# LP pooling over windows of four: the squares of loads 4, 8 and 12 in two parts, with the root and the store of the block before between them

## The chip, the cores and the metric

One core of one Trainium2 chip. The metric is the device time of one execution in microseconds (us), given as the median of several runs. Before the change it is 394.11 us, the median of 3 runs from 394.06 to 394.17.

The engines that matter here: ScalarE (ACT in the profile) takes squares and roots, VectorE (DVE) adds, SyncE (SP) issues loads and the last stores, and 16 DMA engines move the data between HBM and the on-chip memory SBUF. A matrix engine and GpSimd exist and have no part in this kernel.

## What is computed

The input is 32 x 256 x 4096 float32, p is 2 and the window is 4. Each output is the root of the mean of four squares:

```python
out_length = length // kernel_size
for i in range(out_length):
    start = i * kernel_size
    end = start + kernel_size
    window = np.abs(x[:, :, start:end]) ** p
    result[:, :, i] = (np.mean(window, axis=-1)) ** (1.0 / p)
```

134.22 MB are read and 33.55 MB written. Since windows never cross a row's end, the input may be treated as one flat list of numbers that is cut where it suits.

## The kernel before

**Tiling.** The flat input is spread over 128 partitions and cut into 20 loads. Loads 0 to 18 have 13184 columns a partition (`W`, 6592 KB in all), load 19 has 11648. There are three slots for loads in SBUF (`X_SLOTS`): load i lies in slot i mod 3, so load i + 3 can start only when load i's slot has been used up. The sums of a load, a quarter as wide (`R` = 3296 columns), go to one of four places in a tile `ot`, place i mod 4; with four loads' roots in it the whole tile is stored at once. So loads 0-3, 4-7, 8-11 and 12-15 are blocks, each with one store (numbers 0 to 3) of 6592 KB; loads 16 to 18 and load 19 are stored from a free slot as stores 4 and 5.

**Work on one load.** ScalarE squares the slot in place (`square`, L88). VectorE adds columns in pairs in place (`pairs`, L94) and then the pairs (`fours`, L98), into the load's place in `ot`. For loads 4, 8, 12 and 16 the sums go to a PSUM tile `st` instead, so that they need not wait for the store of the block before. ScalarE then takes the root, scaled by 1/4 (`root`, L101), several neighbouring places at a time where it can; for loads 4, 8 and 12 it reads `st` and writes `ot`. Sums of loads 5, 9 and 13 write a place of `ot` that the store of the block before still reads; these wait for that store to land.

**Order.** The order on each engine is the order of the calls, written by hand (`manual_schedule`); only waits are added by the framework. One loop runs over loads 0 to 16. In step i ScalarE squares load i; the table `behind` says which roots follow that square, the table `ahead` which come before it. For i = 4, 8 and 12 `ahead` puts the root of load i - 1 in front of the square, and since this root completes a block, `roots` issues that block's store right behind it on ScalarE's own DMA queue (L115, L85). VectorE then gets the pairs and fours of load i, and SP the issue of load i + 3 (L82), which waits for fours of load i. SP issues everything in order, so a load that waits holds those behind it. Behind the loop, store 3 is issued on SP, load 17 follows the same pattern, and loads 18 and 19 share their squares between VectorE and ScalarE; stores 4 and 5 go out on SP.

`implied` tells the framework that one wait is covered by others and need not be made. It issues nothing.

Of the kernel before, what the change touches and what calls it, by code (L numbers as in the profile page):

```python
# [1 line left out]

# [4 lines left out]


@with_exitstack
def kernel(  # L10
    ctx: ExitStack,
    tc: tile.TileContext,
    x: bass.AP,
    p: float,
    kernel_size: int,
    out: bass.AP,
):

    nc = tc.nc

    assert float(p) == 2.0, "kernel specialized for p == 2"
    k = int(kernel_size)  # L30
    assert k == 4, "kernel specialized for kernel_size == 4"

    P = nc.NUM_PARTITIONS
    fp32 = mybir.dt.float32
    Act = mybir.ActivationFunctionType
    add = mybir.AluOpType.add
    xf = x.rearrange("b c l -> (b c l)")
    of = out.rearrange("b c l -> (b c l)")
    total = xf.shape[0] // P

    W = 13184
    R = W // k
    X_SLOTS = 3
    LAST = total - 19 * W
    widths = [W] * 19 + [LAST]
    n = len(widths)
    assert 0 < LAST <= W and LAST % 16 == 0


    blocks = [[0, 1, 2, 3], [4, 5, 6, 7], [8, 9, 10, 11], [12, 13, 14, 15], [18, 16, 17], [19]]  # L50
    block_of = {i: b for b, group in enumerate(blocks) for i in group}
    block_width = [sum(widths[i] for i in group) for group in blocks]

    x_pool = ctx.enter_context(tc.tile_pool(name="x_pool", bufs=1))
    o_pool = ctx.enter_context(tc.tile_pool(name="o_pool", bufs=1))
    s_pool = ctx.enter_context(tc.tile_pool(name="s_pool", bufs=1, space=bass.MemoryType.PSUM))
    x_tiles = [x_pool.tile([P, W], fp32, name=f"xt{j}") for j in range(X_SLOTS)]
    o_tile = o_pool.tile([P, 4 * R], fp32, name="ot")
    first = o_pool.tile([P, 1], fp32, name="first")
    s_tile = s_pool.tile([P, 4096], fp32, name="st")  # L60
    ctx.enter_context(tc.manual_schedule())

    def rows(flat, b, div):
        at = sum(block_width[:b]) * P // div
        return flat[at:at + block_width[b] * P // div].rearrange("(p w) -> p w", p=P)


    free = x_tiles[17 % X_SLOTS]
    place = {i: o_tile[:, i % 4 * R:(i % 4 + 1) * R] for i in range(16)}
    place[18] = free[:, R:2 * R]  # L70
    place[19] = free[:, 0:LAST // k]
    place[16] = free[:, 2 * R:3 * R]
    place[17] = free[:, 3 * R:4 * R]
    held = [o_tile[:, :]] * 4 + [free[:, R:4 * R], place[19]]

    xs, loads, stores, sums = {}, {}, {}, {}

    def load(i):
        b = block_of[i]
        at = sum(widths[j] for j in blocks[b][:blocks[b].index(i)])  # L80
        xs[i] = x_tiles[i % X_SLOTS][:, 0:widths[i]]
        loads[i] = nc.sync.dma_start(out=xs[i], in_=rows(xf, b, 1)[:, at:at + widths[i]])  # L82

    def store(b, queue):
        stores[b] = queue.dma_start(out=rows(of, b, k), in_=held[b])  # L85

    def square(v):
        return nc.scalar.activation(out=v, in_=v, func=Act.Square)  # L88

    def pairs(v):  # L90

        q = v.rearrange("p (n j) -> p n j", j=k)
        h = v[:, 0:v.shape[1] // 2].rearrange("p (n j) -> p n j", j=2)
        return nc.vector.tensor_tensor(out=h, in0=q[:, :, 0:2], in1=q[:, :, 2:4], op=add)  # L94

    def fours(o, v):
        h = v[:, 0:v.shape[1] // 2].rearrange("p (n j) -> p n j", j=2)
        return nc.vector.tensor_tensor(out=o, in0=h[:, :, 0], in1=h[:, :, 1], op=add)  # L98

    def root(o, s):  # L100
        return nc.scalar.activation(out=o, in_=s, func=Act.Sqrt, scale=1.0 / k)  # L101

    summed = {i: s_tile[:, 0:R] if i in (4, 8, 12, 16) else place[i] for i in range(n)}

    def roots(*group):
        if len(group) == 1:
            root(place[group[0]], summed[group[0]])
        else:
            v = o_tile[:, group[0] % 4 * R:(group[-1] % 4 + 1) * R]
            r = root(v, v)  # L110
            if group[0] in (5, 9):

                implied(r, stores[block_of[group[0]] - 1])
        if group[-1] in (3, 7, 11):
            store(block_of[group[-1]], nc.scalar)  # L115

    def implied(later, earlier):

        tc.declare_no_dep(later.ins, earlier.ins, reason="implied by the other waits")

    for i in range(X_SLOTS):
        load(i)


    ahead = {4: (3,), 8: (7,), 12: (11,)}
    behind = {3: [(0, 1, 2)], 7: [(5, 6), (4,)], 11: [(9, 10), (8,)], 14: [(12,)], 15: [(13, 14)], 16: [(15,)]}

    root(first[:, :], nc.const_aps.tensor(1.0, (P, 1), fp32))
    for i in range(17):
        if i in ahead:  # L130
            roots(*ahead[i])
        s = square(xs[i])
        if i in (3, 7, 11):

            for earlier in sums[i - X_SLOTS]:
                implied(s, earlier)
        for group in behind.get(i, []):
            roots(*group)
        sums[i] = pairs(xs[i]), fours(summed[i], xs[i])
        if i + X_SLOTS < n:  # L140
            load(i + X_SLOTS)

    store(3, nc.sync)
    square(xs[17])
    pairs(xs[17])
    fours(summed[17], xs[17])
    later = {18: 4608, 19: 2000}

    def shared_square(i):
        v = xs[i][:, 0:later[i]]  # L150
        nc.vector.tensor_tensor(out=v, in0=v, in1=v, op=mybir.AluOpType.mult)  # L151
        square(xs[i][:, later[i]:widths[i]])

    def shared_pairs(i):
        implied(pairs(xs[i]), loads[i])

    shared_square(18)
    roots(16)
    roots(17)
    shared_pairs(18)  # L160
    fours(summed[18], xs[18])
    shared_square(19)
    roots(18)
    store(4, nc.sync)
    shared_pairs(19)
    fours(summed[19], xs[19])
    roots(19)
    store(5, nc.sync)


# [1 line left out]
_INS = ['x', 'p', 'kernel_size']  # L172
_OUTS = [((32, 256, 1024), 'float32')]

_NUMBERS = {'p': 2.0, 'kernel_size': 4}


# [26 lines left out]
```

## Time and profile before

| | |
|---|---|
| median of 3 runs | 394.11 us (394.06 to 394.17) |
| the profiled execution's own time | 393.96 us |
| its span (first to last instruction) | 392.2 us |
| ScalarE busy | 274.4 us (70%), 37 instructions |
| VectorE busy | 218.2 us (56%), 42 instructions |
| DMA | 167.77 MB, mean 428 GB/s over the span |
| one square of 13184 columns | 11.19 us |
| pairs, fours of such a load | 7.03 us, 3.59 us |
| root of 3296 columns, from `ot` | 2.95 us |
| ScalarE waiting for loads, in all | 90.9 us, 13 times |
| VectorE waiting for squares, in all | 144.3 us, 18 times |
| VectorE waiting for stores, in all | 17.1 us, 3 times |

An engine's row tells how long it was busy with instructions; issuing a DMA isn't counted. A DMA's row on a queue (SPq, ACTq) marks the issue, and the transfer itself goes on for many microseconds behind it. Landing is when its completion is told. In the rows of time the place in brackets is the engine's idle time before an instruction, and what ended it. Stretches are counted from the span's start.

### The profile page before, as it was taken

What the parts mean: (1) busy time and instruction counts of PE and PEld (TensorE: products, weight loads), DVE (VectorE), ACT (ScalarE), POOL (GpSimd) and SP (SyncE); (2) the same over time, 40 slices, a digit from 0 to 9 for tenths busy, and PEclk for the clock granted to TensorE, in tenths of its full rate; (3) what the DMA queues carried; (4) which work ended last, traced back from release to release, by engine and by line L of the source; (5) the groups of instructions that cost most, each with busy time, mean ns of one, the idle gap of its engine ahead of it and who ended that gap; (6) DMA issues with size and microseconds to landing.
All of it is one profiled execution on the core that took longest, in us unless ns stands there. A gap on an engine that the chain in (4) does not pass through costs nothing.

```text
span 392.2 us, 176 instructions
## 1 busy us (share of the span) xinstructions
DVE 218.2 (56%) x42; ACT 274.4 (70%) x37; POOL 0.2 (0%) x4
## 2 busy tenths in 40 slices
DVE  0008477490593374905942748069418485699980
ACT  1095685979950859799509597995098999969910
POOL 0000000000000000000000000000000000000000
DMA  8999999999999999999999999999999999999997
GB/s 344 430 430 441 436 436 441 436 436 387 430 430 430 430 430 430 430 436 430 446 441 452 446 441 436 430 430 430 430 430 430 430 430 430 430 428 438 430 413 342
DMA packets 3744, 167.77 MB, mean 428 GB/s; under 512 B 416, under 2 KB 416, under 8 KB 416
## 3 DMA queue, kind: packets, MB, share of 16 engines
q1 hardware_dynamic: 3312, 147.52, 87.4%
q10 hardware_dynamic: 432, 20.25, 11.9%
HBM read 134.22 MB, written 33.55 MB: 428 GB/s over the span
## 4 chain that ended last, share of the span: by engine, by line
DMA 43%; ACT 31%; DVE 23%; issue 0%; ACTq 0%; SPq 0%; DVEq 0%
DMA xt<-in_x_dram 43%; ACT xt L88 28%; DVE xt L94 14%; DVE ot L98 5%; DVE xt L98 3%; DVE xt L151 2%; ACT ot L101 2%; ACT xt L101 1%; ACTq L85 0%; SPq L82 0%; DVEq L94 0%
## 5 line engine op out<-in xcount | busy, mean ns | idle before, releaser
L88 ACT ACTIVATE xt<-xt 128x13184 f32<-128x13184 f32 (+2 forms) x20 | 216.7, 10847 | 92.2 <-DMA xt<-in_x_dram 90.9
L94 DVE TENSOR_TENSOR xt<-xt 128x6592 f32<-128x6592 f32 (+1 forms) x20 | 139.7, 6986 | 144.6 <-ACT xt L88 144.3
L98 DVE TENSOR_TENSOR ot<-xt 128x3296 f32<-128x3296 f32 x13 | 46.7, 3592 | 17.5 <-DMA out_dram<-ot 17.1
L101 ACT ACTIVATE ot<-ot 128x3296 f32<-128x3296 f32 (+2 forms) x8 | 37.2, 4656 | 7.0 <-DVE ot L98 7.0
L101 ACT ACTIVATE xt<-xt 128x3296 f32<-128x3296 f32 (+1 forms) x3 | 8.5, 2840 | 8.8 <-DVE xt L98 8.8
L98 DVE TENSOR_TENSOR st<-xt 128x3296 f32<-128x3296 f32 x4 | 14.4, 3600 | 0.1
L98 DVE TENSOR_TENSOR xt<-xt 128x3296 f32<-128x3296 f32 (+1 forms) x3 | 10.4, 3458 | 0.1
L101 ACT ACTIVATE ot<-st 128x3296 f32<-128x3296 f32 x3 | 8.7, 2899 | 0.0
L151 DVE TENSOR_TENSOR xt<-xt 128x4608 f32<-128x4608 f32 (+1 forms) x2 | 7.2, 3593 | 0.0
L101 ACT ACTIVATE xt<-st 128x3296 f32<-128x3296 f32 x1 | 2.9, 2899 | 0.0
L101 ACT ACT_TABLE_LOAD x1 | 1.3, 1283 | 0.7 <-PEq L185 0.7
L101 ACT ACTIVATE first<-const-float32-1.0 128x1 f32<-128x1 f32 x1 | 0.2, 203 | 0.0
L185 POOL MEMSET const-bfloat16-1.0<- 128x1 bf16 x1 | 0.1, 101 | 0.0
L185 POOL MEMSET const-uint8-127<- 128x1 uint8 x1 | 0.1, 101 | 0.0
L185 POOL MEMSET const-float32-0.0<- 128x1 f32 x1 | 0.1, 98 | 0.2 <-issue 0.2
L185 POOL MEMSET const-float32-1.0<- 128x1 f32 x1 | 0.1, 98 | 0.0
## 6 DMA issues: line engine op xcount, KB each, us to landing
xt<-in_x_dram SPq DMA_DIRECT2D x19, 6592.0 KB, 29.7
out_dram<-ot ACTq DMA_DIRECT2D x3, 6592.0 KB, 35.1
out_dram<-ot SPq DMA_DIRECT2D x1, 6592.0 KB, 37.0
xt<-in_x_dram SPq DMA_DIRECT2D x1, 5824.0 KB, 21.9
out_dram<-xt SPq DMA_DIRECT2D x1, 4944.0 KB, 16.1
out_dram<-xt SPq DMA_DIRECT2D x1, 1456.0 KB, 8.2
```

The lines of the kernel that those rows point to most:

```text
L88: return nc.scalar.activation(out=v, in_=v, func=Act.Square)
L94: return nc.vector.tensor_tensor(out=h, in0=q[:, :, 0:2], in1=q[:, :, 2:4], op=add)
L98: return nc.vector.tensor_tensor(out=o, in0=h[:, :, 0], in1=h[:, :, 1], op=add)
L101: return nc.scalar.activation(out=o, in_=s, func=Act.Sqrt, scale=1.0 / k)
L151: nc.vector.tensor_tensor(out=v, in0=v, in1=v, op=mybir.AluOpType.mult)
L185: nc = _bacc.Bacc("TRN2", target_bir_lowering=False, num_devices=1)
```

## The change

For loads 4, 8 and 12 the square is cut in two along its columns. ScalarE squares the first 8812, 8340 or 8160 columns, then takes the root of load i - 1 and issues the store of the block before, and then squares the remaining 4372, 4844 or 5024 columns. Before, the root and the store came first and the square was one instruction. The order on VectorE and SP, the sizes of all DMAs, and every other instruction stay as they are. The added calls of `implied` belong to waits that the cut would otherwise add.

```diff
-    ahead = {4: (3,), 8: (7,), 12: (11,)}
+    ahead = {4: 8812, 8: 8340, 12: 8160}
...
     for i in range(17):
         if i in ahead:
-            roots(*ahead[i])
-        s = square(xs[i])
+            halves = square(xs[i][:, 0:ahead[i]]), roots(i - 1), square(xs[i][:, ahead[i]:W])
+        else:
+            s = square(xs[i])
...
+        if i in (7, 11, 15):
+            implied(s, halves[0])
+            implied(s, halves[2])
         for group in behind.get(i, []):
             roots(*group)
         sums[i] = pairs(xs[i]), fours(summed[i], xs[i])
+        if i in ahead:
+            implied(sums[i][0], loads[i])
+            implied(sums[i][1], loads[i])
         if i + X_SLOTS < n:
             load(i + X_SLOTS)
+            if i in ahead:
+                implied(loads[i + X_SLOTS], loads[i])
...
-        square(xs[i][:, later[i]:widths[i]])
+        return square(xs[i][:, later[i]:widths[i]])
...
-    shared_square(18)
+    s = shared_square(18)
+    implied(s, halves[0])
+    implied(s, halves[2])
```

On ScalarE the order around load 4 becomes, in the built program: square of load 3, roots of loads 0 to 2, first part of the square of load 4, root of load 3, issue of store 0, second part of the square of load 4, square of load 5. The first part waits for load 4, the root for VectorE's sum of load 3, the issue for the root; the second part has no wait of its own. Around loads 8 and 12 the pattern is the same, with the roots of loads 5, 6 and 4 (9, 10 and 8) in front.

## The prediction

> **What bounds the kernel now.** I read the slices of the span first, to see which resource is never idle, then the DMA queues, then the DMA rate by stretches, then the order of time around the first store, and last who waits for whom.
>
> ```profile
> ACT  1095685979950859799509597995098999969910
> ...
> DMA  8999999999999999999999999999999999999997
> GB/s 344 430 430 441 436 436 441 436 436 387 430 430 430 430 430 430 430 436 430 446 441 452 446 441 436 430 430 430 430 430 430 430 430 430 430 428 438 430 413 342
> ...
> q1 hardware_dynamic: 3312, 147.52, 87.4%
> q10 hardware_dynamic: 432, 20.25, 11.9%
> ```
>
> The reader is to see that ScalarE has holes in every group of loads and that the DMA engines have none: the two queues' packets take 87.4 + 11.9 = 99.3% of 16 engines' span. q10 is ScalarE's queue, with stores 0, 1 and 2; everything else is on q1. The kernel is a DMA stream, with compute fitted into its shadow. The same by stretches (columns: stretch, its length, busy time of VectorE, ScalarE and GpSimd, granted clock, DMA share, GB/s):
>
> ```profile
> 4.00:92.00 88.00, 42.47 (x8) 56.78 (x7) 0.00 (x0) 1.00 1.01 435
> 92.00:100.00 8.00, 0.00 (x0) 8.00 (x1) 0.00 (x0) 1.00 1.00 382
> 100.00:372.00 272.00, 167.29 (x33) 205.50 (x28) 0.00 (x0) 1.00 1.00 435
> ```
>
> Outside one stretch of 8 us the rate stands at 435 GB/s. There it is 382, so 8 x (1 - 382/435) = 0.97 us of transfer time is lost. The packet records agree: 20 packets that start between 91 and 98 us take 2.0 to 3.3 us where the usual packet of 52,736 bytes takes 1.947, and the excess over 16 engines is 0.97 us. They begin 0.9 us after the first DMA that ScalarE's queue ever issues, and are nearly all packets of loads. Stores 1 and 2 show none. At 372 us nothing has been lost but this and the start.
>
> Now the work around store 0, in order of time (start, duration, engine, line, operation, idle time before and what ended it):
>
> ```profile
> 77.05 8.43 ACT L101 ACTIVATE ot<-ot 128x9888 f32<-128x9888 f32 x1
> 77.17 7.03 DVE L94 TENSOR_TENSOR xt<-xt 128x6592 f32<-128x6592 f32 x1 [4.94 <-ACT xt L88]
> 84.23 3.59 DVE L98 TENSOR_TENSOR ot<-xt 128x3296 f32<-128x3296 f32 x1
> 87.86 2.95 ACT L101 ACTIVATE ot<-ot 128x3296 f32<-128x3296 f32 x1 [2.38 <-DVE ot L98]
> 90.84 0.38 ACTq L85 DMA_DIRECT2D out_dram<-ot  x1
> 91.27 22.27 ACT L88 ACTIVATE xt<-xt 128x13184 f32<-128x13184 f32 x2 [0.46 <-ACT ot L101]
> ...
> 126.95 3.59 DVE L98 TENSOR_TENSOR ot<-xt 128x3296 f32<-128x3296 f32 x1 [6.36 <-DMA out_dram<-ot]
> 128.82 11.19 ACT L88 ACTIVATE xt<-xt 128x13184 f32<-128x13184 f32 x1 [15.29 <-DMA xt<-in_x_dram]
> 140.05 7.03 DVE L94 TENSOR_TENSOR xt<-xt 128x6592 f32<-128x6592 f32 x1 [9.50 <-ACT xt L88]
> ```
>
> ScalarE idles 2.38 us until VectorE's sum of load 3 is there, takes the root, issues store 0, and only then squares load 4, which landed at 81.5. Later it waits 15.29 us for load 6. VectorE waits 6.36 us for store 0 before it may overwrite load 1's place with the sum of load 5, and 9.50 us more before it has work again. Both engines have slack behind the change; the DMA engines have none.
>
> **The change part by part.** Three places are alike; the first is worked in full.
>
> *Squares in two.* Whole squares give the price by width: 13184 columns 11.19 us, 9648 columns 8.24, 8576 columns 7.35, so 0.832 ns a column. For 8812 columns that is 7.35 + 236 x 0.000832 = 7.55 us, for 4372 it is 3.85: together 11.40, or 0.22 more than whole. At loads 8 and 12 it is 7.16 + 4.25 and 7.01 + 4.40, 11.41 each. Three times 0.22 is 0.65 us more ScalarE work, hidden by the 15.29, 14.74 and 14.71 us of ScalarE waiting for loads 6, 10 and 14; without that cover it would cost 0.65.
>
> *The move.* The first part begins where ScalarE now idles: its roots end at 77.05 + 8.43 = 85.48 and it overlaps the one before by some 0.1, so 85.39 to 92.94. The root follows to 95.79 and the issue of store 0 stands at 95.82 instead of 90.84: **4.98 us later**. The second part runs from about 96.25 to 100.1, where the whole square ended at 102.46: **2.4 us earlier**. At loads 8 and 12 the store goes from 169.29 to 173.93 (4.64 later) and from 247.15 to 251.64 (4.49 later), and the square ends 2.3 earlier. The store is the only DMA that this queue issues there.
>
> *What the earlier square gives.* The sums of load 4 end 2.4 us earlier, so SP issues load 7 at about 110.9 instead of 113.2. But load 6 holds the queue until it lands at 128.8, and load 7 waits there for 15 us already. Likewise for loads 11 and 15. Gain 0; the cover would have to go altogether before the 2.4 us counted.
>
> *What the later store costs.* Issue to landing took 36.0, 35.1 and 34.9 us for the three stores, against 15.6 for a load that has the engines to itself: a store shares them half and half with the loads. So it lands at 95.82 + 36.0 = 131.8, then 209.0 and 286.5. Three things wait for it. VectorE's sum of load 5 (L98) runs 131.9 to 135.5; behind it on VectorE stand the sums of load 6, released by a square that now ends at 140.0 and by the changed shares perhaps 2 us sooner, at about 138. VectorE still has at least 2.5 of its 9.50 us. The slot's next load, number 8, is issued at 130.6 + 5.0 = 135.6; loads 12 and 16 at 208.1 + 4.6 = 212.8 and 285.8 + 4.5 = 290.3. The load ahead of each lands at 144.4, 222.2 and 300.1. So they are queued 8.8, 9.4 and 9.8 us ahead, where it was 13.8, 14.1 and 14.3. To be in time a DMA needs from issue to its first packet 1.0 us on an idle ring (load 0) and 3.3 to 3.8 on a busy one (the stores). I take 3.8, the worst: at least 5.0 us are spare. SP issues in order, and the load behind each is asked for more than 10 us later, so nothing else is held up. Cost 0.
>
> *Which transfers run when.* The same bytes move: what the store doesn't take in the first 5 us, load 5 takes, and lands sooner; later the store takes it back. With packets always waiting on one queue or the other the total is unchanged, so loads 7, 11 and 15 land as before, and all behind load 15 with them: loads 18 and 19 at 346.8 and 360.6, stores 4 and 5 issued at 371.77 and 383.2, the last landing at 391.3.
>
> *The 0.97 us at the first use of ScalarE's queue.* The trace doesn't tell if it belongs to the queue's first DMA or to the moment. Bounds: gone, -0.97; as it is, 0; again at another store as well, +0.97. I take 0, since it comes within 1 us of the first issue and stores 1 and 2 pass without it: the first DMA stays first.
>
> *A rule against the change.* Issuing the store later goes against the Trainium skill, "DMA: Bandwidth & Descriptors", section "Rules for kernel authors", whose line on overlap says to issue a DMA early and wait on it late. By that line at full price the delays would be 4.98 + 4.64 + 4.49 = 14.1 us, and the kernel 408; the row of 99.3% says that no engine is idle to profit from an earlier store, and the sum goes by the row.
>
> Sum against the profiled execution: 393.96 (span 392.2 and 1.76 around it) + 0 + 0 + 0 = 393.96. The median shown is 394.11, 0.15 higher with runs 0.11 apart; I forecast on the median: **394.1 us**.
>
> **The rivals.**
>
> *A, faster: the first-use loss goes.* If the slow packets belong to a store that starts in the midst of a load with another one queued, then issuing at 95.8, near the end of load 5, could spare them: 394.11 - 0.97 = 393.1. For it: they are packets of loads, not of the store. Against it: stores 1 and 2 also start in the midst of loads, without loss.
>
> *B, slower: the queue runs dry between loads.* Load 8 can't be issued before store 0 has landed and VectorE has added for 3.6 us. If load 7 has less left by then than that, the engines empty. It decides from 5.0 us beyond my landing time. Did the store get 0.40 of the engines rather than half, its 15.6 us of work would last 39 us instead of 31.2, landing 7.8 later: 2.8 us dry at each of three places, 394.1 + 8.4 = 402.5. For it: the move uses up a third of the lead. Against it: three stores so far took half, within 1.1 us of each other.
>
> *C, slower by a little: the loss comes twice.* 394.11 + 0.97 = 395.1, if a later issue meets more loads.
>
> *D, the change doesn't do what it says.* The second part could be held by a wait of its own. The built program has none: the first part waits for the load alone, the second for nothing. Were it so all the same, ScalarE's 15 us would take it: 394.1.
>
> **How the numbers follow.** The forecast, with D, gets 0.82, A 0.07, B 0.08, C 0.03. About 0.2% (0.8 us) is what a measurement of this kernel can tell from no change. A passes that bound only when nearly all of the loss goes, so of its 0.07 I count 0.05 as faster; B and C make slower 0.11; same is 0.84. The likeliest case alone has 393.8 to 394.4, the spread of runs and the small changes of rate; the bounds of the one unknown, A and C, widen it to 393.1 to 395.1, and only B is left out.
>
> **What would show it.** ScalarE's row of 8812 columns near 85.4 and its store near 95.8; sums of load 5 waiting some 13 us for the store; load 8 issued near 135.6; load 7 landing near 144.4 as now; 435 GB/s from 100 to 372 us; one stretch of about 380 GB/s, moved to about 97 to 105. I am wrong if a second stretch stands below 430, if load 7 or 8 lands over 1 us late, or if the last load lands over 1 us away from 360.6.

## The result and the profile after

The changed kernel takes 396.20 us, the median of 20 runs, against 394.08 us for the kernel before, also 20 runs: a ratio of 1.0053, with a 95% interval of 1.0041 to 1.0065. It is slower by 2.1 us. The forecast was 394.1 us, no change. As telling as the median is the scatter: the kernel before lies between 393.83 and 394.70, the changed one between 393.44 and 397.86. Of the 141 runs of the kernel before that stand beside this study's experiments, 140 lie between 393.75 and 395.36, and one took 398.12: it isn't wholly free of such scatter.

The profiled execution took 396.01 us with a span of 394.2 us, 2.0 more than before. First the slices and the queues of the changed kernel's page, then its DMA rate by the same three stretches as before (stretch, length, busy VectorE, ScalarE and GpSimd, clock, DMA share, GB/s):

```profile
DMA  8999999999999999999999999999999999999995
GB/s 342 428 428 433 455 439 439 439 444 433 417 433 428 428 433 428 428 428 428 423 439 444 433 449 444 439 433 428 428 428 428 428 428 428 428 454 408 428 447 224
...
q1 hardware_dynamic: 3312, 147.52, 86.8%
q10 hardware_dynamic: 432, 20.25, 11.9%
```

```profile
4.00:92.00 88.00, 42.47 (x8) 59.73 (x6) 0.00 (x0) 1.00 1.00 433
92.00:100.00 8.00, 0.03 (x1) 7.55 (x4) 0.00 (x0) 1.00 1.00 415
100.00:372.00 272.00, 165.90 (x32) 201.24 (x29) 0.00 (x0) 1.00 1.00 434
```

No hole has opened: the rate from 100 to 372 us is 434 GB/s, where it was 435, and the slow stretch at 92 us has become faster, 415 after 382. What stands out is the last slice: 224 GB/s, where it was 342. The transfers run on with part of the engines.

The same place as in the prediction, around store 0, in order of time:

```profile
76.94 8.43 ACT L101 ACTIVATE ot<-ot 128x9888 f32<-128x9888 f32 x1
85.27 7.53 ACT L88 ACTIVATE xt<-xt 128x8812 f32<-128x8812 f32 x1
92.71 2.93 ACT L101 ACTIVATE ot<-ot 128x3296 f32<-128x3296 f32 x1
95.67 0.37 ACTq L85 DMA_DIRECT2D out_dram<-ot  x1
96.09 14.93 ACT L88 ACTIVATE xt<-xt 128x4372 f32<-128x4372 f32 x2 [0.45 <-ACT ot L101]
...
126.61 11.19 ACT L88 ACTIVATE xt<-xt 128x13184 f32<-128x13184 f32 x1 [15.59 <-DMA xt<-in_x_dram]
130.72 3.59 DVE L98 TENSOR_TENSOR ot<-xt 128x3296 f32<-128x3296 f32 x1 [12.65 <-DMA out_dram<-ot]
137.83 7.03 DVE L94 TENSOR_TENSOR xt<-xt 128x6592 f32<-128x6592 f32 x1 [3.52 <-ACT xt L88]
144.27 11.19 ACT L88 ACTIVATE xt<-xt 128x13184 f32<-128x13184 f32 x1 [6.47 <-DMA xt<-in_x_dram]
```

All of this is as forecast: the store 4.8 us later, VectorE waiting 12.65 us for it and still 3.52 us idle behind it, load 7 there at 144.27. The time is lost behind these lines, and no view of engines and waits tells where. The trace's completion records do. Each transfer has 16 of them, one from each DMA engine, and it counts as landed with the last. First, middle (median) and last of the 16 completions, in us:

```
                 before                        changed
           first  middle    last         first  middle    last
load 4     80.51   80.87   81.52         80.60   80.99   81.40
load 8    159.30  159.66  159.96        158.75  159.11  159.81
load 11   221.56  221.92  222.24        221.01  221.36  223.37
load 15   299.40  299.76  300.08        298.85  299.21  301.54
load 19   359.95  360.31  360.62        359.39  359.74  362.57
store 5   390.68  391.03  391.33        390.13  390.47  393.37
```

In the changed kernel the middle engine ends 0.56 us *sooner* than before, and the last one 2.04 us later; the second-last ends at 390.81. One engine of sixteen has fallen behind, in steps: between loads 8 and 11, while store 1 ran, its lag behind the middle one grew by 1.3 us, and it grew further while stores 2 and 3 ran. The packet records show the same step. A full load is 128 packets of 52,736 bytes, 8 for each of the 16 engines, and a packet usually takes 1.947 us. Four packets of loads start at 180.82, 185.03, 189.15 and 193.44 us and take 2.27, 2.18, 2.34 and 2.36; each but the first starts 1.94 us after the end of the one before, the time of one usual packet, as on one engine that moves a packet of load and a packet of store in turn. Together they take 1.36 us too long. Up to the end of this trace the lag isn't made up, and nothing shows that other engines take packets over. A square that waits for a load waits for the last engine. In the mean over 16 engines 2 us of one of them are an eighth of a microsecond, which is why the rates above show nothing.

In what follows medians and ranges are over all runs of a kernel; the ratio of a comparison leaves out runs more than 1.5% above the kernel's fastest, and where the scatter itself is the finding the range says more.

### The profile page after: what moved, and what is told of

Its sections match the earlier page's. It is cut to its first block, busy times and chain, and to the rows that moved or that the text cites. A ratio compares the mean times of both kernels' runs of the same rounds, so it can differ in the third digit from the quotient of the medians.

```text
span 394.2 us, 179 instructions
## 1 busy us (share of the span) xinstructions
DVE 218.2 (55%) x42; ACT 274.3 (70%) x40; POOL 0.2 (0%) x4
## 4 chain that ended last, share of the span: by engine, by line
DMA 45%; ACT 35%; DVE 18%; issue 0%; ACTq 0%; SPq 0%; DVEq 0%
DMA xt<-in_x_dram 45%; ACT xt L88 28%; DVE xt L94 11%; ACT ot L101 6%; DVE ot L98 3%; DVE xt L98 3%; DVE xt L160 2%; ACT xt L101 1%; ACTq L85 0%; SPq L82 0%; DVEq L94 0%
## 5 line engine op out<-in xcount | busy, mean ns | idle before, releaser
L88 ACT ACTIVATE xt<-xt 128x13184 f32<-128x13184 f32 (+8 forms) x23 | 217.2, 9457 | 101.3 <-DMA xt<-in_x_dram 100.0
```

## The experiments

The first theory (P) was the packets' phase: the later store meets the engines at another point of their 1.95 us packet period, they all take it up together, and an engine falls out. Its rivals were the cut (S), the lateness of the store (L), and the nearness of the store's issue to a load's landing (B).

**The cut alone.** Root and store stay in front of both parts.

```diff
-            halves = square(xs[i][:, 0:ahead[i]]), roots(i - 1), square(xs[i][:, ahead[i]:W])
+            roots(i - 1)
+            halves = square(xs[i][:, 0:ahead[i]]), None, square(xs[i][:, ahead[i]:W])
```

> Squares of loads 4, 8 and 12 in two parts as in the change, but root and store in front of both, as before; the store's issue stays at 90.8, 169.3 and 247.2 us. Theory P (the store's issue falls at another point of the DMA engines' packet period of 1.95 us; they then all switch between load and store together and one engine falls behind): 394.1 +- 0.4, runs within 1 us, completions of the last transfer within 0.8 us over the 16 engines. Rival S (the cut itself costs): 395.5 to 396.5, runs 3 us apart. Rival L (a later store costs, in proportion to its delay): 394.1.

Measured: 394.03 us (393.84 to 394.41, 11 runs), ratio 1.0001 [0.9992, 1.0009]. The cut costs nothing. S falls.

**Stores later still, by half a packet period and by a whole one.**

```diff
-    ahead = {4: 8812, 8: 8340, 12: 8160}
+    ahead = {4: 9982, 8: 9510, 12: 9330}
+    ahead = {4: 11152, 8: 10680, 12: 10500}
```

> The change with first parts of 9982, 9510 and 9330 columns: every store 0.97 us later still, half a packet period. P: the engines split over load and store as in the kernel before, 394.1 +- 0.5, spread of runs under 1.5 us. S: 396.2. L (2.1 us for 4.7 us of delay, so 0.45 us per us): 396.6. Rival B (the store comes within 1.5 us of a load's landing): between 394.1 and 396.2, since the issue now stands 0.3 to 1 us behind the landing.

> The change with first parts of 11152, 10680 and 10500 columns: every store 1.95 us later still, a whole packet period, so the same phase as the change. P: 395.5 to 396.7, runs 2 us or more apart, one engine over 1.5 us behind the others at the last transfer. S: 396.2. L: 397.1. B: 394.1, since the store is issued 1 to 2 us behind a load's landing.

Measured: 394.40 us (393.90 to 395.70, 12 runs), ratio 1.0012 [1.0004, 1.0021], and 394.29 us (393.90 to 395.38, 11 runs), ratio 1.0007 [0.9999, 1.0016]. Lateness is no cost, so L falls; and a whole period later is not like the change, so P falls as I had put it. B has it right both times, though with half a period its range (394.1 to 396.2) was so wide that P's 394.1 fits as well.

**Squares whole and in front.** Stores later again, by nearly two periods, with no cut.

```diff
+        s = square(xs[i])
         if i in ahead:
             roots(*ahead[i])
-        s = square(xs[i])
```

> Squares of loads 4, 8 and 12 whole and in front of root and store: stores 3.7 to 4.2 us later than in the change, close to two packet periods, with no cut. P: like the change, 395.3 to 396.8 with runs 2 us or more apart, if the phase comes out the same. S: 394.1. L: 398.0. B: 394.1.

Measured: 394.69 us (393.72 to 396.00, 11 runs), ratio 1.0013 [1.0003, 1.0024]. A little slower and scattered, but not the change's 2.1 us: between what P and B had said.

**One place at a time, and the change again.** A second pair of theories: T, each store whose packets all engines take up together costs its part; F, the changed store 0 passes with a smaller loss (5.6 engine-microseconds of excess between 90 and 130 us instead of 15.5; the excess is what packets of 52,736 bytes take beyond 1.947 us, summed over all engines), and this loss is what aligns the engines. In each kernel the other two places are as before.

```diff
-    ahead = {4: 8812, 8: 8340, 12: 8160}
+    ahead = {4: 8812}
...
+            if i in (8, 12):
+                roots(i - 1)
             s = square(xs[i])
```

> Only load 4's square is cut, with root 3 and store 0 between the parts; loads 8 and 12 as in the kernel before. Theory T (an engine is lost while a store that all engines take up together runs beside loads; each such store adds its part, by the completions of the change's trace 0.3 us at store 0, 1.3 at store 1, 0.3 at store 2 and 0.5 at store 3): 393.5 to 394.5, since store 0 gives little and its first-use loss is 0.6 us smaller. Rival F (the smaller first-use loss leaves the 16 engines unaligned, and all stores behind it suffer): 395.2 or more, runs 2 us apart.

> Only load 8's square is cut, with root 7 and store 1 between the parts. T: 395.0 to 395.7, the largest of the three. F: 394.1, since store 0 is issued as before and the engines are aligned by its loss.

> Only load 12's square is cut, with root 11 and store 2 between the parts. T: 394.3 to 394.9. F: 394.1.

> The changed kernel itself once more, for a second trace and runs on the same chip: 396.2, runs 393.4 to 397.9. By T and F alike one engine is over 1 us behind the others at the last transfer; by T the steps stand at stores 1 to 3, by F the engine that is late at the end is already late at load 6.

Measured: load 4 alone 398.58 us (393.77 to 402.35, 12 runs), load 8 alone 394.57 us (394.16 to 395.08, 11 runs), load 12 alone 394.20 us (393.88 to 394.89, 11 runs), the change again 396.55 us (395.91 to 396.68, 5 runs). T's order is wrong. Of the three places alone store 0's costs nearly everything, and the change is even better than its part at load 4 alone, so the three don't add up. With load 4 alone eight of twelve runs lie at 398 to 402 and four at 393.8 to 394.6. In the change's second trace the last engine is 2.45 us behind the middle one at load 6 already, as F had said, where in the first trace most of the lag came with store 1: the same kernel loses it at different stores.

**Store 0 again, store 0 sooner, and the queue warmed.** Now F against B, and against U: that the loss at 92 us is the plain cost of a queue's first use. For the warm-up, ScalarE's queue gets a load of 16 bytes a partition at the start.

```diff
+    warm = o_pool.tile([P, 4], fp32, name="warm")
...
+    nc.scalar.dma_start(out=warm[:, :], in_=rows(xf, 0, 1)[:, 0:4])
```

> The kernel with only load 4's square cut, once more, for a trace of one of its slow executions. Theory F (store 0 issued at 95.7 us passes with a small first-use loss, and the 16 engines go on unaligned; one or a few of them are then slowed at every stretch in which a store runs): runs from 393.8 to 402, most above 398; in a slow execution the median engine finishes as early as in the others, the last one 4 us or more behind, in steps at stores. Rival Q (a queue runs dry or an engine waits): all 16 engines late alike.

> Load 4 cut at 7642 columns: store 0 issued 0.97 us sooner, at 94.7 us; stores 1 and 2 as before. F: the result follows the size of the loss at store 0: if the excess over 16 engines is above 0.6 us, 394.1 +- 0.4; if below 0.4, over 395 with runs 2 us apart. Rival B (the issue must not fall within 1.5 us before the completions of load 5 at 96.2 to 97.0): 396 or more. Rival L (lateness): 396 or more.

> The kernel before with one small load (16 bytes a partition) on ScalarE's queue at the start, into a tile of its own, so that the queue's first use is over before store 0. Stores stand at 90.8, 169.3 and 247.2 us. F: the loss of 0.97 us at store 0 is gone, but nothing aligns the engines: median engine 0.9 us earlier, the last one 1 us or more behind it, 394 to 397 with runs 2 us apart. Rival U (first use is a plain cost, and what hurts in the change is the time of its store): 393.1 +- 0.3, runs within 1 us.

> The changed kernel with the same small load at the start. F: 396 or more with runs 2 us apart. U: 395.5 to 396.2, as the change less its small loss of 0.3 us. If the first use itself is what upsets the engines at 95.7 us: 393.1 to 393.6, runs within 1 us.

Measured: load 4 alone once more 397.98 us (394.01 to 402.06, 12 runs), with the profile on a quick execution of 394.01, so that its trace doesn't decide; cut at 7642 columns 400.96 us (400.00 to 401.63, 4 runs); the kernel before with a warmed queue 394.24 us (393.98 to 394.47, 11 runs), ratio 1.0003 [0.9994, 1.0011]; the change with a warmed queue 396.08 us (395.58 to 396.19, 5 runs).

Two theories end here. In the warmed kernel before, the packets between 90 and 130 us still have 14.3 engine-microseconds of excess, against 15.5: the loss at store 0 isn't a first use of the queue, so U falls; its 395.5 to 396.2 for the change with a warmed queue was met all the same. And with store 0 at 94.8 us the excess between 90 and 130 us is 32.0, the time 401: a large loss doesn't save the run. From 91 to 98 us alone it is 5.3 there, which leaves F a way out; the worst case below, with 12.2 in that stretch and 404.22 us, closes it, and F falls. B had said 396 or more and stands.

**Time without a cut, and the window's edges.** Store 0 is delayed with roots of 800 columns into an unused part of PSUM, all else as in the kernel before:

```diff
+        if i == 4:
+            for _ in range(7):
+                root(s_tile[:, R:4096], o_tile[:, 0:4096 - R])
         if i in ahead:
             roots(*ahead[i])
```

The other three are the kernels with one cut, at other widths: `{4: 6470}`, `{4: 9400}` and `{8: 7170}`.

> The kernel before, with seven roots of 800 columns into an unused part of PSUM on ScalarE in front of root 3, so that store 0 is issued near 94.8 us; no square is cut, stores 1 and 2 as before. Theory B (what counts is the time of store 0's issue against the end of load 5, whose completions stand at 96.2 to 97.1 us): 399 to 402, some engines 3 us or more behind at the last transfer. Rival S (the cut, or the root between its parts): 394.1.

> Load 4 alone cut, at 6470 columns: store 0 issued near 93.8 us, 2.4 us before the first completion of load 5 and as far past the kernel before's time as it is short of the change's. B: between 394 and 401, and the window's early edge; if 394.1, the window is under 2 us wide. F (alignment): 394.1 where the excess at store 0 is above 0.6 us.

> Load 4 alone cut, at 9400 columns: store 0 issued near 96.2 us, at load 5's first completion, half-way between the change (95.7, slow) and 0.97 us later (96.7, 394.4). B: between 394.4 and 398, runs 2 us apart or less: the late edge.

> Load 8 alone cut, at 7170 columns: store 1 issued near 173.0 us, 2 us before load 9's first completion, as only_4_early has it for store 0 and load 5. If every store has the window: 397 or more. If it is store 0's alone, or store 0's passage at the old time arms the engines against it: 394.1 to 394.7.

Measured: 401.33 us (400.38 to 403.29, 5 runs) for the uncut kernel with a late store; 404.22 us (403.22 to 406.24, 5 runs) at 6470 columns; 394.78 us (393.83 to 402.89, 12 runs) at 9400; 402.31 us (400.63 to 402.74, 5 runs) for store 1 at 7170. B has the uncut kernel and store 1 right; its 394 to 401 at 6470 columns was too low, and its runs 2 us apart at 9400 were 9 us apart. The uncut kernel in order of time:

```profile
77.31 8.43 ACT L101 ACTIVATE ot<-ot 128x9888 f32<-128x9888 f32 x1
85.77 6.09 ACT L101 ACTIVATE st<-ot 128x800 f32<-128x800 f32 x7
91.79 2.93 ACT L101 ACTIVATE ot<-ot 128x3296 f32<-128x3296 f32 x1
94.75 0.38 ACTq L85 DMA_DIRECT2D out_dram<-ot  x1
95.18 11.19 ACT L88 ACTIVATE xt<-xt 128x13184 f32<-128x13184 f32 x1 [0.45 <-ACT ot L101]
```

Nothing differs from the kernel before but the seven short roots, which put the store at 94.75 for 90.84 and the square of load 4 at 95.18 for 91.27. It costs 7.3 us. In the kernel cut at 7642 columns store 0 is issued at the same time, but this square ends sooner than before, and it takes 400.96: so it isn't the square. That is the cause shown: **when the store is issued**, not the cut or the order of root and square. Store 1 has such a window too.

The worst case, store 0 at 93.6 us, has enough lost to be seen in the mean rate (by stretches, columns as above):

```profile
100.00:132.00 32.00, 17.55 (x3) 10.94 (x1) 0.00 (x0) 1.00 0.99 382
132.00:172.00 40.00, 24.73 (x5) 30.77 (x4) 0.00 (x0) 1.00 1.00 431
172.00:212.00 40.00, 17.75 (x4) 25.22 (x3) 0.00 (x0) 1.00 1.01 407
212.00:250.00 38.00, 22.92 (x5) 30.77 (x4) 0.00 (x0) 1.00 0.99 429
250.00:292.00 42.00, 19.56 (x4) 25.22 (x3) 0.00 (x0) 1.00 1.01 419
292.00:338.00 46.00, 25.62 (x6) 42.69 (x6) 0.00 (x0) 1.00 1.00 432
```

Stores 0, 1 and 2 run in the first, third and fifth of these stretches: 382, 407 and 419 GB/s. Between them loads alone run at 429 to 432. In the kernel before the three stretches with stores read so:

```profile
100.00:132.00 32.00, 21.24 (x4) 16.71 (x3) 0.00 (x0) 1.00 0.99 428
172.00:212.00 40.00, 21.24 (x4) 25.26 (x3) 0.00 (x0) 1.00 1.02 442
250.00:292.00 42.00, 21.24 (x4) 27.29 (x3) 0.00 (x0) 1.00 1.02 442
```

The DMA share reads 0.99 to 1.02 in both: an engine with a slow packet is a busy engine. Packets of 52,736 bytes that usually take 1.947 us took up to 3.9 us there; their excess between 90 and 130 us is 41.9 engine-microseconds on loads and 27.8 on the store. Here it isn't one engine that is late: the middle completion of store 5 is at 399.23 us, 8.2 later than in the kernel before, and the last only 1.4 behind it.

**The early edge, and which rows.** The last two ask how near the kernel before stands to the window, and whether it is bare time or a matter of which rows the store moves while the load moves which (R). In the second, store 0 stands at the worst time and goes out in two halves, the upper partitions first.

```diff
-    ahead = {4: 8812}
+    ahead = {4: 4600}
```

```diff
+        if b == 0:
+            queue.dma_start(out=rows(of, b, k)[64:P, :], in_=held[b][64:P, :])
+            stores[b] = queue.dma_start(out=rows(of, b, k)[0:64, :], in_=held[b][0:64, :])
```

> Load 4 alone cut, at 4600 columns: store 0 issued near 92.2 us, 4 us before load 5's first completion, between the kernel before (90.8, 394.1) and the worst place so far (93.6, 404.2). Theory B with an edge near 93: 394.1 to 395. If the edge is nearer to the kernel before: 396 or more.

> Store 0 at 93.6 us as in the worst case (404.2), but as two stores, first of partitions 64 to 127 and then of 0 to 63, so that each engine moves other rows than the load's at the same moment; bytes and the first issue's time are the same, with one more DMA issue on ScalarE's queue (0.4 us). Theory B as bare time: 402 to 405. Theory R (what hurts is that a store moves the rows that the load moved two packets before): 394 to 396.

Measured: 394.12 us (393.91 to 400.89, 12 runs) for store 0 at 92.3 us, ten runs under 394.6 and two at 400 to 401, with the profile on one of these two; 406.96 us (405.44 to 408.56, 6 runs) with swapped rows at 93.8 us, above B's 402 to 405 too. R gets no support: other rows at the same time are no better, though the records don't tell which rows each engine moved, and two half stores aren't one.

All places together. The first completion of load 5, where the store leaves it alone, is at 96.2 us; that of load 9 at 175.0, of load 13 at 252.7. Where all three stores are moved the row gives store 0's time.

| store | issued at, us | against the load's first completion | kernel | median (range), us |
|---|---|---|---|---|
| 0 | 90.8 | -5.4 | before | 394.08 (393.83 to 394.70) |
| 0 | 92.3 | -3.9 | load 4 alone, 4600 | 394.12 (393.91 to 400.89) |
| 0 | 93.6 | -2.6 | load 4 alone, 6470 | 404.22 (403.22 to 406.24) |
| 0 | 94.8 | -1.4 | not cut, seven roots | 401.33 (400.38 to 403.29) |
| 0 | 94.8 | -1.4 | load 4 alone, 7642 | 400.96 (400.00 to 401.63) |
| 0 | 95.7 | -0.5 | load 4 alone, 8812 | 398.58 (393.77 to 402.35) |
| 0 to 2 | 95.7 | -0.5 | the change | 396.20 (393.44 to 397.86) |
| 0 | 96.1 | -0.1 | load 4 alone, 9400 | 394.78 (393.83 to 402.89) |
| 0 to 2 | 96.7 | +0.5 | half a period later | 394.40 (393.90 to 395.70) |
| 0 to 2 | 97.8 | +1.6 | a period later | 394.29 (393.90 to 395.38) |
| 0 to 2 | 99.4 | +3.2 | whole squares first | 394.69 (393.72 to 396.00) |
| 1 | 173.0 | -2.0 | load 8 alone, 7170 | 402.31 (400.63 to 402.74) |
| 1 | 174.0 | -1.0 | load 8 alone, 8340 | 394.57 (394.16 to 395.08) |
| 2 | 251.6 | -1.1 | load 12 alone, 8160 | 394.20 (393.88 to 394.89) |

The distance alone doesn't settle the cost: stores 1 and 2 at -1.0 and -1.1 us cost 0.5 us or less, where store 0 costs 4.5 at -0.5 and about 7 at -1.4. And loads follow each other every 15.6 us, so the end of the load is only a mark: its start, or the number of packets still queued, would serve as well.

No version beats the kernel before. The quickest single run of the study is the change's 393.44 us.

## Why the prediction was wrong, point by point

*The parts on ScalarE and VectorE* were right, but for store 2, which the lag itself made 1.1 us late. Squares of 8812 columns took 7.53 us for a forecast 7.55, the store was issued at 95.67 for 95.82, 173.76 for 173.93 and 252.73 for 251.64, and landed at 130.62, 209.72 and 287.89 for 131.8, 209.0 and 286.5. Load 8 was issued at 134.37 for 135.6. VectorE was left 3.52 us for at least 2.5. The 15.6 us beside the stores' 36.0 was misread: it is the distance of two landings, where load 0 took 18.45 from issue to landing.

*"What the later store costs ... Cost 0."* The queues never ran dry: loads 8, 12 and 16 were issued 9.9 us before the load ahead landed, for 8.8 to 9.8 forecast. So rival B of the prediction didn't happen either, and the count of waits held. Only the 3.3 to 3.8 us from a store's issue to its first packet was too little, 3.6 to 4.3 in the change.

*"Which transfers run when"* is the step that failed. It said that with packets always waiting the total is unchanged, "so loads 7, 11 and 15 land as before". Load 7 did, at 144.24. Loads 11 and 15 landed at 223.37 and 301.54, 1.1 and 1.5 us late, and load 19 at 362.57, 2.0 late, the sign of being wrong that the prediction had named. The step treated 16 engines as one server whose packets all take the same time. The records show 16 that finish apart: in the changed kernel packets of 52,736 bytes took 1.95 to 2.60 us behind 90 us, the middle engine came in 0.56 us sooner, and the last one, 2.04 us later, decides. The Trainium skill, "DMA: Bandwidth & Descriptors", section "Why a DMA increments its semaphore by 16 and not by 1", says that the engines finish independently and that only the full count means that the data has landed. The records above agree: 16 completions for each transfer, 0.65 us apart at the last one before, 3.24 us after. I read that as a rule on correctness; here it sets the time.

*"The 0.97 us at the first use"* was misread. The packets' excess was there, but warming the queue left it at 14.3 of 15.5 engine-microseconds. Nor does it belong to the moment of 90.8 us: in the three kernels with all stores later (96.7, 97.8 and 99.4 us) it is 12.1 to 12.5, and behind 130 us their slow packets add at most 0.9. So it comes once, with the first store. In the change it shrank to 5.6, that is 0.35 us an engine, and the middle engine did gain 0.56 us. Rival A was right about that and wrong about the end, where one engine stood 2.9 us behind the middle one.

*"The rule against the change"*, to issue early, was rightly not priced by the delay. Neither its full price of 14.1 us nor lateness as such appears: the kernels with stores 1 to 4 us later than the change's are quicker than the change. But the forecast's answer, that no idle engine could profit, was no proof that an engine couldn't lose.

*The rivals* all priced the queue's emptiness, a fixed loss or a missing wait. None let one engine diverge, though the trace of before held the hint: 20 packets far over their usual time at the very place where the change moved a store.

*The chances*: slower had 0.11. With the profile as it stood I could not have priced the window, but a move of the only event at which packets had slowed deserved a wider upper end than one more loss of 0.97 us.

Open is why store 0, issued 0.5 to 2.6 us ahead of a load's completions, slows packets of loads and, in the worst cases, of the store for long after, when one issued 5 us ahead or just behind doesn't; why stores 1 and 2 bear 1 us ahead; why the three stores of the change together cost less than store 0 alone; and why one kernel takes either 394 or 398 to 402 us at the window's edges. How the change's 2.1 us divide among its three stores isn't shown. Which physical engine lags can't be told: the records carry no number of it.

## What to carry to other kernels

When DMA is the bound, a mean rate or busy share of 99% says nothing of the slowest of the 16 engines: read the spread of a transfer's completions, and see whether it grows from transfer to transfer. When a store on a second queue is moved within a stream of loads, its time relative to the end of the load in flight is part of the change; sweep it in steps of a microsecond, each with a dozen runs, since one width can hit a window that its neighbours miss. Runs that scatter over several microseconds where those before mostly kept within one are a reason to look at the completions, even if the median looks harmless: here that was how the lag showed.

## What the runs showed of the hardware that was not expected

A store of 6.75 MB issued 2.6 us before a load's first completion costs 10 us (404.22 against 394.08), though the same bytes move and the DMA engines' busy share stays at 0.99 to 1.01. The damage can last: in the change's trace the last engine is 0.7 us behind the middle one at load 8, 2.0 at load 11, 2.3 at load 15 and 2.9 at store 5; in its second trace 2.45 at load 6, 3.7 at load 15 and 3.1 at store 5. The loss of 15.5 engine-microseconds at the kernel before's first store isn't a first use of the queue (14.3 with the queue warmed), and the changed kernel, where it was 5.6, wasn't quicker for it.
